# Bias lines by single-pass products, and the order of the opening, of branch A's first scores and of two later stages

## The chip, the cores and the metric

The kernel runs on one core of a Trainium2 chip. The metric is the device time of one execution in microseconds, as the median of three runs. The profile that is quoted is one further execution, taken by the hardware profiler. Engines are named as the profile names them: PE (TensorE, matrix products), PEld (its weight loads), DVE (VectorE), ACT (ScalarE), POOL (GpSimd) and SP (SyncE, which here only issues DMAs).

## What is computed

One encoder layer over two inputs, 1024 rows (the sample) and 256 rows (the prompt) of width 1024. Cut to what matters:

```python
h = _rmsnorm(x, g_mix)
z = h @ w_in                       # q, k, v of two branches, and two gates
o_a, _ = _banded_attention(qa, ka, va, A_WINDOW, 1, rel_bias[:, :A_HEADS], sink)
o_b = _dilated_mixture(qb, kb, vb, rel_bias[:, A_HEADS:])
merged = gates[:, :, 0] * (o_a @ w_branch_a) + gates[:, :, 1] * (o_b @ w_branch_b)
x = x + merged @ w_out
h = _rmsnorm(x, g_mlp)
return x + jnp.square(jax.nn.relu(h @ w_up)) @ w_down
```

A final RMSNorm follows. Branch A is attention in a window of 128 with a sink; it has 8 heads. Branch B mixes three dilated windows with 4 heads each. Both add a bias to the logits, which depends only on the distance of query and key: a table of 32 buckets by 20 heads (`rel_bias`) is looked up by the bucket of the distance.

## The kernel before, in words

Everything runs in one program whose order is written out by hand: within `manual_schedule` each engine carries out its instructions in the order in which the program issues them. Python generators (`turn`, `line`, `fill`, `side` and so on) are advanced step by step with `next`, so that the work of one engine is laced into that of another. DMAs are issued mostly on SP's queue, in program order; a DMA whose destination is not yet free holds up those behind it. Tiles of 4 KB per partition come from a pool of 33 slots ("m"), weights from one of 10 ("w").

**Products.** A float32 operand is split into a high part (rounded to fp32r by ACT, `hi`) and a low part (the rest, by DVE, `lo`). A product of two such operands is three fp32r products: hi x hi, hi x lo and lo x hi, each a single pass on PE. `split` issues both halves at once; `split_steps` yields between ACT's and DVE's. Products of plain float32 tiles are possible too (`tab`, `ones`, `ident` below); the trace shows two PE records for each of those, and one for an fp32r product. `mm3` and `six` (lines 186 to 193 and 351 to 360) issue the three products over all blocks of the inner dimension; `six` with `late=True` first does all products of the two high parts, then those with the low part of the moving operand, and last those with the low part of the stationary operand.

**The stages, in order.**

1. The opening (lines 670 to 905). Row tiles of x are loaded, squared (`square`, ACT), scaled by 1/rms and g_mix (`scale`, DVE), transposed on PE (`turn`), and split. g_mix arrives as a single row and is spread over all partitions by a product with a row of ones (line 816; the result is `g`). Some transposes of the identity into an unused bank stand ahead of and behind it (lines 812 and 813). Tiles 0 and 1 use `g` straight from its bank (`scale_first`, line 825). The value columns of w_in are split piece by piece (`split_v`, line 699), and `values` (line 766) multiplies: first tiles 0 and 1 together, then tile after tile. In that loop the DVE work of a tile is the low halves, the copies out, and the combinations that the next stage needs.
2. The projections (lines 806 to 1075), by pairs of column blocks (`pair`), with a seven-product scheme for two-by-two blocks (`seven`, `prompt`). Between them runs branch B's attention (`attention_b`), and in the hooks of the first six pairs the bias lines: `line` (line 287) multiplies a table tile `tab` (128 x 128 float32, rows 0 to 31 are rel_bias, row 32 is -1e30, the rest zero) with a matrix of zeros and ones (`hot`), which gives the bias per head for each distance (one bias line of 512, two of 384 and three of 256 columns). It is stored and read back with a skew.
3. Branch A (lines 1075 to 1400). 40 tiles (4 units of two heads, 10 row tiles each) pass through scores, maxima, exponentials, transposes and products with the values. Between them PE does the rest of the gate projection in small steps (`fill`, made by `logits`, line 1155): a step is four products of 512 columns or eight of 256. Line 1323 does 18 such steps ahead of the first score. The blocks whose left side is `h21` need tiles that were stored and are loaded back (`scr_h`) shortly before. `load_unit` loads q, k and v of a unit; it is called for the next unit at the unit's tile 0 (line 1329). `merges_of` loads branch B's rows (`r`, from `scr_b`) on SP's queue and merges them on DVE (lines 1178 to 1245).
4. The merge with the gates (lines 1400 to 1445): 48 jobs. Each loads gate values six jobs ahead (`load_gate`), applies the sigmoid three jobs ahead (ACT) and multiplies on DVE. In four jobs `fetch` loads the next weight on SP's queue (line 1424).
5. w_out, the second norm, the up projection, and the down projection (`Down`, lines 1605 to 1815). The down projection has 28 steps; each takes five row blocks (t = 0 to 4), with twelve products of 512 columns per block. The left sides (`uhi`, `ulo`, `up`) and right sides (`dhi`, `dlo`) of a step are split by ACT and DVE during the step before. Line 1788 calls `six` with `late` in the very first block only.

Of the kernel before, what the change touches and what calls it, by code (L numbers as in the profile page):

```python
# [10 lines left out]
F32 = mybir.dt.float32  # L11
# [4 lines left out]
P = 128  # L16
# [6 lines left out]
HD = 64  # L23
# [73 lines left out]
def encoder_kernel(  # L97
# [156 lines left out]
    nsink = const.tile([P, AH], F32, name="nsink")  # L254
    tab = const.tile([P, P], F32, name="tab")
    nc.gpsimd.memset(tab, 0.0)
# [21 lines left out]
    scr_u = [dram.tile([P, 7, 4, TH], F32, name=f"scr_u{g}") for g in range(FF // P // 8)]  # L278
    lines = {}

    def toeplitz(i, cols, first, lo):
# [4 lines left out]

    def line(i, make):

        h0, n, length, _ = LINES[i][3:]
        first = sum(x[5] for x in LINES[:i])  # L290
        hs = make("z")[:, :length]
        nc.gpsimd.memset(hs, 0.0)
        nc.gpsimd.dma_start(hs[: BUCKETS + 1, :], hot[:, first : first + length])
        yield
        yield
        ps = bank("pv", "line")
        nc.tensor.matmul(ps[:, :length], tab, hs, start=True, stop=True)
        ln = make("z")[:NH, :length]
        nc.vector.tensor_copy(ln, ps[:NH, :length])
        d = dram.tile([n, length], F32, name=f"line{i}")  # L300
        nc.gpsimd.dma_start(d, ln[h0 : h0 + n, :])
        wide = dram.tile([P, n, length], F32, name=f"wide{i}")
        nc.gpsimd.dma_start(wide, d[:, :].unsqueeze(0).to_broadcast([P, n, length]))
        lines[i] = wide
        yield
# [365 lines left out]
    with ExitStack() as pre:  # L671
# [6 lines left out]
        gm = slot("gm")  # L678
        gm_row = slot("row")[:1, :]
        ones = small.tile([1, P], F32, name="ones", tag="ones", bufs=1)  # L680
        nc.vector.memset(ones, 1.0)
        NV = (512, 384)
# [16 lines left out]
        def split_v(v, i):  # L699
            if v == 0:  # L700
                hi, lo = wslot("vhi", (P, 2, 512), F32R), wslot("vlo", (P, 2, 512), F32R)
            else:
                hi, lo = own("v2", (P, 2, 384), F32R, 8), own("v2", (P, 2, 384), F32R, 8)
            split(hi, lo, v_raw.pop((v, i)))
            v_parts[v, i] = hi, lo

        def square(t):
# [14 lines left out]
        def turn(t):  # L722
# [19 lines left out]
            for (hi, _), cols, src in jobs:  # L742
                nc.scalar.activation(hi[:, :, cols], src, AF.Copy)
            for (hi, lo), cols, src in jobs:
                nc.vector.tensor_tensor(lo[:, :, cols], src, hi[:, :, cols].bitcast(F32), op=ALU.subtract)
# [37 lines left out]

        nc.scalar.dma_start(gm_row, g_mix)
        load_x(0)
# [25 lines left out]
        for h in range(3):  # L811
            for _ in range((4, 0, 6)[h]):
                nc.tensor.transpose(idle[:, :P], ident, ident)
            if h < 2:
                ps = bank(("mm", "pv")[h], "g")
                nc.tensor.matmul(ps, ones, gm_row[:, 512 * h : 512 * h + 512], start=True, stop=True)
                spread_gm.append(ps)
# [12 lines left out]
        square(1)  # L830
        scale_first(1)
        next(turns[0])
        split_v(0, 0)
        next(turns[1])
        next(turns[1])
        split_v(0, 1)
        square(2)
        split_v(0, 2)
        for h in range(2):
            nc.vector.tensor_copy(gm[:, 512 * h : 512 * h + 512], spread_gm[h])  # L840
        scale(2)
        next(turns[0], None)
        split_v(0, 3)
        square(3)
# [18 lines left out]
        for t in range(2, NT):  # L863
            if t + 1 < NT:
                next(turns[t + 1])
                next(turns[t + 1])
            if t + 3 < NT:
                square(t + 3)
            if t + 2 < NT:
                scale(t + 2)  # L870
            if t + 1 < NT:
                next(turns[t + 1], None)
            if t < 6:
                split_v(1, t - 2)
            if t > 7:
                next(b0)
            ps = bank("mm", "v")
            values(t, 0, ps)
            evac(t, 0, ps)

        def more():
# [368 lines left out]
    if True:  # L1250
# [70 lines left out]
        for name, shape, n in (("bias", (P, 2, 3 * P), 2), ("pt", (P, 6, P), 2), ("s", (P, 2, 3 * P), 4)):  # L1321
            a3(name, shape, n)
        steps_of(fill, 18)
        for i in range(0, len(order) + 4, 2):
            for j in range(2):
                pieces = []
                if i < len(order):
                    u, t = order[i + j]
                    if t == 0 and u < 3:
                        units[u + 1] = load_unit(u + 1), load_bias(u + 1, lambda name, shape: a3(name, shape, 2))  # L1330
# [83 lines left out]
        for i, (x, b, c) in enumerate(jobs):  # L1414
# [8 lines left out]
            open_gate(i + 3)  # L1423
            if i in (1, 4, 22, 26):
                fetch()
            elif i in (5, 8, 33, 35):
                w_as[(5, 8, 33, 35).index(i)] = weight(0)
            elif i in (38, 40, 42, 44):
                prepare()
# [174 lines left out]
    class Down:  # L1604
# [4 lines left out]
        def make(self, name, shape=(P, 2, 512), dt=F32):  # L1609
            return self.late.tile(list(shape), dt, name=name, tag="l4", bufs=8)  # L1610
# [165 lines left out]
        def go(self):  # L1776
            with tc.tile_pool(name="down", bufs=1) as self.late:
                for s, (n, g) in enumerate(JOBS):
# [6 lines left out]
                    for t in range(5):  # L1785
                        ps = self.bank(n, t, g % 2 == 0)
                        six(ps, self.rights[n, g], [self.at(n, g, t, k) for k in range(4)],
                            g % 2 == 0 and n not in (2, 3), g % 2 == 1 and n not in (1, 2), late=s + t == 0)
                        next(side, None)
# [171 lines left out]
```

## Time and profile before

| | |
|---|---|
| median of three runs | 1675.86 us (1675.23 to 1676.54) |
| profiled execution | 1676.28 us |
| its span, first to last instruction | 1673.6 us |
| PE busy | 1660.3 us (99%) |
| PEld busy | 1408.6 us (84%) |
| DVE busy | 980.7 us (59%) |
| ACT busy | 733.3 us (44%) |
| POOL busy | 429.4 us (26%) |
| granted PE clock, mean | 0.999 |

The span starts with the first instruction; about 2.7 us of the profiled execution lie outside it. The stages by time: the opening runs to about 116 us, the projections to 525, branch A to 664, the gates' merge to about 750, w_out and the up projection to 1284, the down projection to the end. A row of the order of time reads: start in us, duration in us, engine, line, operation, destination <- sources, shape, count; in brackets stands how long the engine had been idle before it and what it waited for. Rows of the same line in sequence are merged (x4). A matmul's own duration contains its latency; two neighbours overlap, and what one costs is the distance between the starts. In the list of waits the columns are: waiting engine, tile and line, then what it waited for, with the sum in us, how often, and the longest. Rows of the chain of waits (the work that ended last, followed back from the end) hold start, length and what it was.

### The profile page before, as it was taken

What the parts mean: (1) busy time and instruction counts of PE and PEld (TensorE: products, weight loads), DVE (VectorE), ACT (ScalarE), POOL (GpSimd) and SP (SyncE); (2) the same over time, 40 slices, a digit from 0 to 9 for tenths busy, and PEclk for the clock granted to TensorE, in tenths of its full rate; (3) what the DMA queues carried; (4) which work ended last, traced back from release to release, by engine and by line L of the source; (5) the groups of instructions that cost most, each with busy time, mean ns of one, the idle gap of its engine ahead of it and who ended that gap; (6) DMA issues with size and microseconds to landing.
All of it is one profiled execution on the core that took longest, in us unless ns stands there. A gap on an engine that the chain in (4) does not pass through costs nothing.

```text
span 1673.6 us, 27177 instructions
## 1 busy us (share of the span) xinstructions
PE 1660.3 (99%) x10342; PEld 1408.6 (84%) x10342; DVE 980.7 (59%) x1662; ACT 733.3 (44%) x1586; POOL 429.4 (26%) x399
## 2 busy tenths in 40 slices
PE   9999999999999999999999999999999999999998
PEld 7898888888888888888888888888888888888886
DVE  7634554554452586666578545455457867666575
ACT  7232553544442677544275333333334333333345
POOL 0210122111111222000100456555555412314140
PEclk9999999999999999999999999999999999999999
DMA  6315666664546953545121543343347845633333
GB/s 239 118 55 123 169 186 179 197 195 138 152 120 170 270 177 120 205 139 201 38 89 59 160 161 124 118 161 130 112 160 269 293 131 179 205 101 107 119 119 126
DMA packets 228116, 255.86 MB, mean 153 GB/s; under 512 B 30184, under 2 KB 158652, under 8 KB 227858
## 3 DMA queue, kind: packets, MB, share of 16 engines
q1 hardware_dynamic: 218224, 228.00, 43.1%
q0 software_dynamic: 8384, 23.51, 4.4%
q10 hardware_dynamic: 1378, 2.63, 0.4%
q8 instruction: 81, 1.33, 0.3%
q14 instruction: 49, 0.40, 0.1%
HBM read 168.58 MB, written 90.73 MB: 155 GB/s over the span
## 4 chain that ended last, share of the span: by engine, by line
PE 93%; DMA 3%; DVE 1%; issue 1%; ACT 1%; SPq 0%; POOL 0%; DVEq 0%; ACTq 0%; POOLq 0%
PE dn L357 21%; PE x L357 20%; PE mm L191 14%; PE z L357 10%; PE v L773 6%; PE pv L357 5%; PE y L357 5%; PE mm L357 5%; PE pv L594 1%; PE pv L1140 1%; PE sc L549 1%; PE pt L337 1%; PE tr L346 1%; DMA q<-scr_qa 1%; DMA r<-scr_b 1%
## 5 line engine op out<-in xcount | busy, mean ns | idle before, releaser
L357 PE MATMUL dn<-dhi,ulo 128*128 128x512 f32 x448 | 173.7, 389 | 0.7 <-DVE ulo L185 0.7
L357 PE MATMUL dn<-dhi,uhi 128*128 128x512 f32 x448 | 173.8, 389 | 0.0
L357 PE MATMUL dn<-dlo,uhi 128*128 128x512 f32 x448 | 173.8, 389 | 0.0
L357 PE MATMUL x<-chi,wlo 128*128 128x512 f32 x424 | 166.7, 393 | 0.0
L357 PE MATMUL x<-clo,whi 128*128 128x512 f32 x424 | 165.7, 391 | 0.0
L357 PE MATMUL x<-chi,whi 128*128 128x512 f32 x424 | 165.0, 389 | 0.0
L316 DVE TENSOR_TENSOR wlo<-ta,whi 128x1024 fp32r<-128x1024 f32 x30 | 55.2, 1839 | 160.3 <-ACT whi L314 160.3
L316 DVE TENSOR_TENSOR wlo<-raw,whi 128x1024 fp32r<-128x1024 f32 x60 | 89.4, 1489 | 89.4 <-ACT whi L314 89.4
L391 POOL TENSOR_TENSOR tb<-raw 128x512 f32<-128x512 f32 x16 | 21.1, 1318 | 338.1 <-DMA raw<-in_w_up_dram 212.3
L615 POOL DMA_DIRECT2D scr_b<-o x72 | 39.1, 547 | 250.0 <-ACT o L606 196.0
L357 PEld LDWEIGHTS dn<-dhi,ulo 128*128 128x128 f32 x448 | 84.1, 188 | 18.7 <-DVE ulo L185 1.2
L357 PEld LDWEIGHTS dn<-dlo,uhi 128*128 128x128 f32 x448 | 84.1, 188 | 17.4
L357 PEld LDWEIGHTS dn<-dhi,uhi 128*128 128x128 f32 x448 | 84.0, 188 | 17.3
L185 DVE TENSOR_TENSOR ulo<-uraw,uhi 128x1024 fp32r<-128x1024 f32 x56 | 90.1, 1628 | 10.9 <-ACT uhi L184 10.9
L357 PEld LDWEIGHTS x<-chi,wlo 128*128 128x128 f32 x424 | 79.8, 188 | 17.2 <-issue 1.5
L357 PEld LDWEIGHTS x<-chi,whi 128*128 128x128 f32 x424 | 79.6, 188 | 17.0
L357 PEld LDWEIGHTS x<-clo,whi 128*128 128x128 f32 x424 | 79.8, 188 | 15.0 <-DVE clo L316 0.4
L1643 POOL TENSOR_TENSOR t<-raw,t 128x1024 f32<-128x1024 f32 x16 | 46.9, 2949 | 144.1 <-DMA raw<-in_w_down_dram 144.1
L1799 DVE TENSOR_TENSOR v<-v,dn 128x512 f32<-128x512 f32 x90 | 59.5, 681 | 40.5 <-PE dn L357 37.6
L565 ACT ACTIVATE s<-s,st 128x128 f32<-128x128 f32 (+1 forms) x120 | 52.0, 435 | 49.3 <-DVE st L561 49.2
L357 PE MATMUL dn<-dhi,up 128*128 128x512 f32 x224 | 73.5, 389 | 0.0
L357 PE MATMUL z<-chi,wlo 128*128 128x512 f32 x184 | 71.9, 391 | 0.0
(354 smaller groups left out, 4599.3 us busy)
## 6 DMA issues: line engine op xcount, KB each, us to landing
scr_u<-u SPq DMA_DIRECT2D x112, 320.0 KB, 2.6
uraw<-scr_u SPq DMA_DIRECT2D x56, 512.0 KB, 4.4
raw<-in_w_in_dram SPq DMA_DIRECT2D x33, 512.0 KB, 5.6
raw<-in_w_up_dram SPq DMA_DIRECT2D x32, 512.0 KB, 5.5
raw<-in_w_down_dram SPq DMA_DIRECT2D x28, 512.0 KB, 5.9
sg<-scr_g SPq DMA_DIRECT2D x32, 256.0 KB, 5.3
uraw<-scr_u SPq DMA_DIRECT2D x28, 256.0 KB, 4.3
v<-scr_v SPq DMA_DIRECT2D x96, 64.0 KB, 2.7
```

What stands on the lines that cost most here:

```text
L185: nc.vector.tensor_tensor(lo, src, hi.bitcast(F32), op=ALU.subtract)
L191: nc.tensor.matmul(ps, a, b, start=i == 0, stop=i == len(seq) - 1)
L316: nc.vector.tensor_tensor(lo, src, hi.bitcast(F32), op=ALU.subtract)
L337: nc.tensor.transpose(ps[:, HD * k : HD * k + HD], src[r, :], ident[r, r])
L346: nc.tensor.transpose(ps[:, P * i : P * (i + 1)], xn[t][:, P * k : P * (k + 1)], ident)
L357: nc.tensor.matmul(ps, a, b, start=first and i == 0, stop=last and i == len(seq) - 1, skip_group_check=True)
L391: eng.tensor_tensor(tb[:, 0], b12, b11, op=ALU.subtract)
L565: nc.scalar.activation(d, d, AF.Exp, bias=st[:, x, h : h + 1], accum_out=st[:, x, 2 + h : 3 + h])
L615: nc.gpsimd.dma_start(scr_b[first : first + step * (nq - 1) + 1 : step, i, g, :], o[p0 : p0 + nq, c + x, :])
L773: nc.tensor.matmul(ps[:, :n], a, b, start=k == 0 and j == 0, stop=k == KC - 1 and j == 2)
L1643: (eng or nc.gpsimd).tensor_tensor(o, a, b, op=ALU.subtract)
L1799: nc.vector.tensor_tensor(v, v, ps, op=ALU.add)
```

## The change

Eight things change.

- **Bias lines.** After tile 2 of the opening `tab` is split into `tab_hi` and `tab_lo` (two constants). `line` multiplies both with `hot`, whose tile is now declared fp32r: two single-pass products that accumulate in one bank, in place of one float32 product. `tab` itself becomes one of the 33 slots.
- **g_mix.** The row is loaded into the last partition of a full tile, whose other partitions DVE clears with two memsets. The product uses the last column of the identity, broadcast, in place of the row of ones, so it is 128 x 128 by 128 x 512 and not 1 x 128 by 1 x 512.
- **Warm-up.** The identity products around it are now plain products and no transposes, and 3 and 2 instead of 4 and 6.
- **Order of the opening.** The high half of the first value weights is issued ahead of the high halves of tile 0; the low half stands after two of tile 0's four low halves; the other two come after tile 1's transposes.
- **Fill.** 16 instead of 18 steps ahead of branch A's first score.
- **Units.** The next unit and its bias are loaded at tile 4 and no longer at tile 0.
- **Fetch.** The fourth fetch of the merge stands in job 31 and no longer in job 26.
- **Down projection.** `late` holds for the first row block of every step.

```diff
-    tab = const.tile([P, P], F32, name="tab")
+    tab = slot("tab")[:, :P]
...
+    tabs = [const.tile([P, P], F32R, name=name) for name in ("tab_lo", "tab_hi")]
...
-        hs = make("z")[:, :length]
-        nc.gpsimd.memset(hs, 0.0)
+        hs = make("z", (P, 512), F32R)[:, :length]
+        nc.gpsimd.memset(hs.bitcast(F32), 0.0)
...
-        nc.tensor.matmul(ps[:, :length], tab, hs, start=True, stop=True)
+        for i, t in enumerate(tabs):
+            nc.tensor.matmul(ps[:, :length], t, hs, start=i == 0, stop=i == 1)
...
-        gm_row = slot("row")[:1, :]
-        ones = small.tile([1, P], F32, name="ones", tag="ones", bufs=1)
-        nc.vector.memset(ones, 1.0)
+        gm_row = slot("row")
+        nc.scalar.dma_start(gm_row[P - 1 :, :], g_mix)
+        nc.vector.memset(gm_row[:HD, :], 0.0)
+        nc.vector.memset(gm_row[HD : P - 1, :], 0.0)
+        last_one = ident[:, P - 1 :].to_broadcast([P, P])
...
-            split(hi, lo, v_raw.pop((v, i)))
             v_parts[v, i] = hi, lo
+            return split_steps(hi, lo, v_raw.pop((v, i)))
...
-            for (hi, lo), cols, src in jobs:
+            for i, ((hi, lo), cols, src) in enumerate(jobs):
+                if (t, i) == (0, 2):
+                    yield
                 nc.vector.tensor_tensor(lo[:, :, cols], src, hi[:, :, cols].bitcast(F32), op=ALU.subtract)
...
-        nc.scalar.dma_start(gm_row, g_mix)
...
-            for _ in range((4, 0, 6)[h]):
-                nc.tensor.transpose(idle[:, :P], ident, ident)
+            for _ in range((3, 0, 2)[h]):
+                nc.tensor.matmul(idle[:, :P], ident, ident, start=True, stop=True)
             if h < 2:
                 ps = bank(("mm", "pv")[h], "g")
-                nc.tensor.matmul(ps, ones, gm_row[:, 512 * h : 512 * h + 512], start=True, stop=True)
+                nc.tensor.matmul(ps, last_one, gm_row[:, 512 * h : 512 * h + 512], start=True, stop=True)
...
         scale_first(1)
+        first_v = split_v(0, 0)
+        next(first_v)
         next(turns[0])
-        split_v(0, 0)
+        run(first_v)
         next(turns[1])
+        next(turns[0])
         next(turns[1])
...
+            if t == 2:
+                split(tabs[1], tabs[0], tab)
...
-        steps_of(fill, 18)
+        steps_of(fill, 16)
...
-                    if t == 0 and u < 3:
+                    if t == 4 and u < 3:
                         units[u + 1] = load_unit(u + 1), load_bias(u + 1, lambda name, shape: a3(name, shape, 2))
...
-            if i in (1, 4, 22, 26):
+            if i in (1, 4, 22, 31):
                 fetch()
...
-                            g % 2 == 0 and n not in (2, 3), g % 2 == 1 and n not in (1, 2), late=s + t == 0)
+                            g % 2 == 0 and n not in (2, 3), g % 2 == 1 and n not in (1, 2), late=t == 0)
```

The other callers of `split_v` now run its generator at once, which is what they did before.

More of the change, by code (lines that the diff above doesn't have):

```diff
@@ L285, in toeplitz, with line @@
         return bass.AP(a.tensor, a.offset + length * lo + zero + first, [[n * length - 1, P], [length, 2], [1, cols]])
-    def line(i, make):
-        h0, n, length, _ = LINES[i][3:]
-        first = sum(x[5] for x in LINES[:i])
-        hs = make("z")[:, :length]
-        nc.gpsimd.memset(hs, 0.0)
+    def line(which, make):
+        h0, n, length, _ = LINES[which][3:]
+        first = sum(x[5] for x in LINES[:which])
+        hs = make("z", (P, 512), F32R)[:, :length]
+        nc.gpsimd.memset(hs.bitcast(F32), 0.0)
         nc.gpsimd.dma_start(hs[: BUCKETS + 1, :], hot[:, first : first + length])
@@ L296, in line @@
         ps = bank("pv", "line")
-        nc.tensor.matmul(ps[:, :length], tab, hs, start=True, stop=True)
+        for i, t in enumerate(tabs):
+            nc.tensor.matmul(ps[:, :length], t, hs, start=i == 0, stop=i == 1)
         ln = make("z")[:NH, :length]
         nc.vector.tensor_copy(ln, ps[:NH, :length])
-        d = dram.tile([n, length], F32, name=f"line{i}")
+        d = dram.tile([n, length], F32, name=f"line{which}")
         nc.gpsimd.dma_start(d, ln[h0 : h0 + n, :])
-        wide = dram.tile([P, n, length], F32, name=f"wide{i}")
+        wide = dram.tile([P, n, length], F32, name=f"wide{which}")
         nc.gpsimd.dma_start(wide, d[:, :].unsqueeze(0).to_broadcast([P, n, length]))
-        lines[i] = wide
+        lines[which] = wide
         yield
@@ L831, in encoder_kernel @@
         scale_first(1)
+        first_v = split_v(0, 0)
+        next(first_v)
         next(turns[0])
-        split_v(0, 0)
+        run(first_v)
         next(turns[1])
+        next(turns[0])
         next(turns[1])
-        split_v(0, 1)
+        run(split_v(0, 1))
         square(2)
-        split_v(0, 2)
+        run(split_v(0, 2))
         for h in range(2):
@@ L842, in encoder_kernel @@
         next(turns[0], None)
-        split_v(0, 3)
+        run(split_v(0, 3))
         square(3)
@@ L873, in encoder_kernel @@
             if t < 6:
-                split_v(1, t - 2)
+                run(split_v(1, t - 2))
             if t > 7:
```

## The prediction

> **What bounds the kernel now.** I read the page first, then who TensorE waits for, then the order of time at each place that the change touches.
>
> ```profile
> span 1673.6 us, 27177 instructions
> PE 1660.3 (99%) x10342; PEld 1408.6 (84%) x10342; DVE 980.7 (59%) x1662; ACT 733.3 (44%) x1586; POOL 429.4 (26%) x399
> ```
>
> ```profile
> ...
> PE sc L1098 <- DVE m L1100: 1.0, 1, 1.0
> PE v L773 <- ACT vhi L184: 0.8, 1, 0.8
> PE dn L357 <- DVE ulo L185: 0.7, 1, 0.7
> PE mm L191 <- DMA hlo<-scr_h: 0.7, 1, 0.7
> ...
> PE mm L191 <- DVE sg L1442: 0.2, 1, 0.2
> ```
>
> TensorE (PE) is busy for 1660.3 of 1673.6 us, so there are two ways to be faster: give it less to do, or remove one of its few waits. The second fence has the rows of its list of waits that matter here (us in total, how often, longest); together they are 3.4 us, and all that PE is not busy is 13.3. So this change can't bring tens of us; each of its parts is aimed at one of these rows or at work on PE. A change of under 0.2% (3.35 us) is about what a measurement of this kernel can't tell from none.
>
> **Opening.** The order of time on PE, ScalarE (ACT) and VectorE (DVE):
>
> ```profile
> 2.52 3.77 PE L816 MATMUL g<-row,ones 1*128 1x512 f32 x4
> 7.55 2.76 PE L346 MATMUL tr<-ident,xn 128*128 128x128 f32 x16
> ...
> 12.40 1.19 PE L773 MATMUL v<-vlo,hhi 128*128 128x512 f32 x4
> 19.80 1.03 PE L346 MATMUL tr<-ident,xn 128*128 128x128 f32 x8
> ```
>
> ```profile
> 6.94 0.29 ACT L712 ACTIVATE sd<-ss,eps 128x1 f32<-128x1 f32 x1
> 8.65 0.66 ACT L743 ACTIVATE hhi<-tr 128x256 fp32r<-128x256 f32 x2 [1.42 <-PE tr L346]
> 10.03 1.06 ACT L184 ACTIVATE vhi<-vraw 128x1024 fp32r<-128x1024 f32 x1
> ```
>
> ```profile
> 0.86 0.17 DVE L681 MEMSET ones<- 1x128 f32 x1
> 6.17 1.41 DVE L825 SCALAR_TENSOR_TENSOR xn<-xt,rs,g 128x512 f32<-128x512 f32 x2
> 9.34 1.58 DVE L745 TENSOR_TENSOR hlo<-tr,hhi 128x256 fp32r<-128x256 f32 x4 [0.26 <-ACT hhi L743]
> 11.12 1.23 DVE L185 TENSOR_TENSOR vlo<-vraw,vhi 128x1024 fp32r<-128x1024 f32 x1 [0.19 <-ACT vhi L184]
> 15.47 1.23 DVE L185 TENSOR_TENSOR vlo<-vraw,vhi 128x1024 fp32r<-128x1024 f32 x1 [0.67 <-ACT vhi L184]
> ...
> 18.00 1.28 DVE L717 SCALAR_TENSOR_TENSOR xn<-xt,rs,gm 128x1024 f32<-128x1024 f32 x1
> ```
>
> ACT stands idle for 1.42 us before its hhi copies at 8.65, and then does vhi behind them at 10.03. The change issues vhi first, so it falls into that hole: from the end of sd (6.94 + 0.29 = 7.23) to about 8.3. PE's first products then need only the hhi of tiles 0 and 1, and no longer wait the 0.8 of the list. On DVE the change puts vlo after two of the four hlo: they take 1.58 / 4, about 0.4 each, from 9.34 to 10.1, and vlo ends at 10.1 + 1.23 = 11.3 in place of 12.35. So the second group of products starts at about 11.35 and not at 12.40: 1.05 us earlier.
>
> Not all of that stays. Behind it DVE does the other two hlo (to 12.1), four hlo of tile 1 (1.6, to 13.7), a vlo (to 14.9), then the vlo that stood at 15.47 behind a wait of 0.67. Its vhi comes earlier too, as one 1.06 activation ahead of it has moved, so the wait shrinks and the vlo ends at about 16.5 in place of 16.70. The copies and the scaling behind it, which end today at 18.00 + 1.28 = 19.28, end at about 19.1. Meanwhile PE would be ready for the transposes of tile 2 at 19.80 - 1.05 = 18.75, so DVE becomes the one that is late, by 0.3 or 0.4. I keep 0.7 of the 1.05.
>
> The g products (the row g_mix spread over 128 partitions) now need two memsets of 1024 columns on DVE, queued behind eps; nothing waits for DVE before 6.17, apart from g. The only DVE memset shown takes 0.17 for 128 columns. The bounds are that fixed 0.17 a piece if length cost nothing, and eight times it, 1.36, if everything scales; the vlo (1.23 for 1024 columns) is the nearest row of that length, but reads two operands, and I take 1.0. They end between 1.2 and 3.6, on my value at 2.9. Today g starts at 2.52 and ends at 6.29, and its second half is first read by the second half of the operation at 6.17 (at about 6.9). A start at 2.9 ends at 6.7: free. At 3.6 it costs 0.5. [...]
>
> The warm-up instructions around g become full fp32 products, and fewer. They are not on the path, which runs from the x tiles over ACT and DVE. But the transposes at 7.55 take 2.76 for 16 (0.173 each) and at 19.80 1.03 for 8 (0.129): the PE clock is still low there. That is a rival below. Opening: -0.7, between -1.3 and +0.3.
>
> After t = 2 the tile `tab` is split: one ACT and one DVE operation of 128 columns, under 0.4 each (the 256-column copies and differences above); PE has 24 products of tile 3 ahead of it, so 0, or 0.4 if that cover is gone. `tab` also takes one of 33 shared slots until then; between -0.2 and +0.5, I take 0.
>
> **Bias lines.** Six products with the table, 2 x 512, 4 x 384 and 6 x 256 columns as the trace counts two records for each:
>
> ```profile
> L297 PE MATMUL line<-z,tab x12: 377/483/595, 132.1 to 279.1; 128*128 128x256 f32 x6, 128*128 128x384 f32 x4, 128*128 128x512 f32 x2
> ```
>
> ```profile
> 278.64 1.02 PE L297 MATMUL line<-z,tab 128*128 128x512 f32 x2
> ...
> 279.74 0.40 PE L357 MATMUL z<-hlo,whi 128*128 128x512 f32 x1
> ```
>
> ```profile
> 24.48 5.46 PE v L773 x24
> ...
> 121.17 2.87 PE mm L357 x24
> ```
>
> The pair of 512 starts at 278.64, one ordinary product follows (left out), and the next starts at 279.74: 1.10 us for the pair and one ordinary product, which takes 5.46 / 24 = 0.228. So the pair costs 0.87, or 1.70 ns a column. All six have 512 + 2 x 384 + 3 x 256 = 2048 columns: 3.5 us. Two fp32r products each cost 2 x 0.228 at 512 columns, 2 x 2.87 / 24 = 0.24 at 256, and about 0.35 at 384: 0.46 + 0.70 + 0.72 = 1.9. PE is never idle around them, so the difference is the gain: -1.6, between -1.3 and -1.9. The memset, the loads of `hot` and the stores stay in their order on POOL.
>
> **Branch A's first scores.** The two waits of this stage, and what stands behind them:
>
> ```profile
> 551.51 0.40 PE L191 MATMUL mm<-hhi,wlo 128*128 128x512 f32 x1
> 552.61 0.50 PE L191 MATMUL mm<-hlo,whi 128*128 128x512 f32 x1 [0.70 <-DMA hlo<-scr_h]
> ```
>
> ```profile
> 566.53 0.38 PE L1098 MATMUL sc<-kk,q 128*128 128x256 f32 x1 [1.01 <-DVE m L1100]
> ```
>
> ```profile
> 564.30 0.16 DVE L1191 TENSOR_TENSOR mm__6203<-r 128x4 f32<-128x4 f32 x1 [2.71 <-DMA r<-scr_b]
> ```
>
> ```profile
> 550.74 3.57 SPq L435 DMA_DIRECT2D q<-scr_qa  x4
> 554.35 4.73 SPq L449 DMA_DIRECT2D qp<-scr_qa  x4
> 559.62 2.33 SPq L1181 DMA_DIRECT2D r<-scr_b  x3
> ```
>
> From product to product there should be 0.228; at 551.51 it is 1.10, so that loss is 0.87; the second I count with its 1.01. The first: the fill work reaches the columns that are reloaded (`hlo`) before they have landed. With 16 and not 18 steps ahead of the scores, two steps of eight 256-column products (8 x 0.12 = 0.96 each) are left to stand between the first scores, so two more groups of four score products (0.18 each, an estimate between 0.12 and 0.228 for their 384 columns) come ahead of the first product with `hlo`: about 1.4 us later: the wait goes, -0.9. The second: DVE stood for 2.71 us at 564.30 for `r`, and its maxima, for which PE's score banks wait, are queued behind. The load of `r` was issued at 559.62, behind eight loads of the next unit (550.74 to 559.08) on SP's queue. Moved from t = 0 to t = 4, they stand behind the first two `r`, which then land some 8 us earlier, before DVE asks at 564.30 - 2.71 = 561.6: -1.0. Unit 1 itself is then issued at about 552 to 562 and its scores come at 576. Together -1.9, between -2.1 and 0.
>
> **Later.** In the merge, `fetch` goes from job 26 to job 31:
>
> ```profile
> 732.16 0.38 SPq L221 DMA_DIRECT2D raw<-in_w_out_dram  x1
> ```
>
> ```profile
> 736.16 1.31 ACT L1378 ACTIVATE sg<-sg,bg 128x256 f32<-128x256 f32 x3 [8.32 <-DMA sg<-scr_g]
> ```
>
> This fetch stood on SP's queue until 732.16, and the gate loads behind it left ACT idle for 8.32. Past it, five more gate loads go first. PE shows 0.2 of it (its list, `sg`): -0.2. In the down projection the products with `ulo` go last in the first row block of every step:
>
> ```profile
> 1597.11 0.39 PE L357 MATMUL dn<-dhi,up 128*128 128x512 f32 x1
> 1598.23 0.50 PE L357 MATMUL dn<-dhi,ulo 128*128 128x512 f32 x1 [0.74 <-DVE ulo L185]
> ```
>
> ```profile
> 1594.76 4.55 DVE L185 TENSOR_TENSOR ulo<-uraw,uhi 128x1024 fp32r<-128x1024 f32 x2
> ```
>
> 1598.23 - 1597.11 - 0.228 = 0.9. The two `ulo` are done at about 1598.2 and 1599.3. Eight products (1.82) now stand ahead of the first and ten (2.28) ahead of the second, so PE asks at 1597.34 + 1.82 = 1599.2 and 1599.6: -0.9. Other steps have no wait, and the reordering costs nothing there.
>
> **Sum.** 0.7 + 1.6 + 1.9 + 0.2 + 0.9 = 5.3 us. The profiled execution took 1676.28, of which 1673.6 is its span; that is 0.42 above the median of 1675.86. So 1676.28 - 5.3 = 1671.0 beside it, and 1670.6 as a median.
>
> **The rivals.**
> The waits of branch A only move. With the loads of units 2 and 3 later, another `r` stands behind them; for: PE has little slack there. Then 1.9 is missing: 1672.5. Chance 0.17.
>
> More comes. If the clock is granted one step earlier, g's 3.77 and the 16 transposes (2.76, against 2.06 at the later rate) shrink, so that DVE's chain starts 0.5 earlier; the opening then keeps its whole 1.05, the lines their 1.9 and branch A its 2.1. [...] The trace so far shows only the two rates. That is 0.5 + 0.35 + 0.3 + 0.2 = 1.35 more: 1669.2. Chance 0.15.
>
> Slower: unit 2's loads come too late.
>
> ```profile
> 570.23 6.25 SPq L435 DMA_DIRECT2D q<-scr_qa  x4
> ```
>
> ```profile
> 603.67 0.28 PE L1098 MATMUL sc<-kk,q 128*128 128x256 f32 x1
> ```
>
> ```profile
> SPq L1181 <- DVE z L1199: 8.7, 1, 8.7
> ```
>
> Today unit 2's loads end at 576.5 and its first score is at 603.67, some 27 us later. If SP first meets the 8.7 us wait of a later `r` and then issues them from 591 on, with the same 14.5 us of issue (from behind `r`, 559.62 + 2.33 = 561.95, to 576.5) and 4.7 to land (as `r`: 559.62 to 564.30), they are there at 610, while PE, some 3 us ahead by then, asks at about 600.5: 1670.6 + 9.5 = 1680.1. It decides once the first of them is issued after 581. Against: today SP issues them at 562 without such a wait, 41 us ahead of need. Chance 0.06.
>
> **Numbers.** Forecast 0.62, so the predicted time is 1670.6. The range is 1668.0 to 1674.0: at the low end the second rival with the opening's bound (0.6 more) and 0.6 for the spread of the three runs, at the high end the first with the opening at +0.3 and half a microsecond of that spread; some 0.15 to 0.2 is outside. Faster by over 0.2% means under 1672.5: most of the forecast, the second rival and nearly half of the first, 0.77. Within 0.2%: 0.17. Slower: 0.06.
>
> **What would show it.** Right: the second group of v products at 11.3 to 11.7; twelve line products in about half the time; no wait for `hlo` near 551, none of DVE for `r` near 564, none for `ulo` near 1592 to 1597. Wrong: g ending after 7.2, transposes of tile 2 still at 19.8, a new wait of PE for kk or q, or DVE waiting for another `r`.

## The result, and the profile after

| | before | after |
|---|---|---|
| median, timed side by side | 1675.68 us (1675.23 to 1679.03, six executions) | 1667.54 us (1666.65 to 1668.34, six executions) |
| ratio | | 0.9948 (95% interval 0.9935 to 0.9961) |
| profiled execution / its span | 1676.28 / 1673.6 us | 1668.34 / 1665.2 us |

The gain is 8.1 us. The forecast was 5.3 and its range reached down to 1668.0, so the sign was right and the size too small. First the head of the profile's page after, then the whole list of what PE waits for (sum in us, how often, longest).

```profile
span 1665.2 us, 27194 instructions
PE 1655.0 (99%) x10342; PEld 1407.0 (84%) x10342; DVE 976.1 (59%) x1664; ACT 734.2 (44%) x1587; POOL 429.5 (26%) x399
```

```profile
PE idle L818 <- POOL ident masks.py:199: 1.5, 1, 1.5
PE tr L348 <- DVE xn L830: 0.5, 1, 0.5
PE tr L348 <- ACT hhi L747: 0.3, 1, 0.3
```

Of the waits that the prediction quoted none is left: no `hlo`, no maxima `m`, no `vhi`, no `ulo`, no `sg`. Where the 8.4 us of the span went is read from the start of the same instruction in both orders of time, stage by stage:

| first PE instruction of the stage | before | after | ahead by | gained in the stage before it | forecast |
|---|---|---|---|---|---|
| x after the value stage | 115.52 | 114.05 | 1.47 | opening 1.5 | 0.7 |
| last group of z products (its first) | 518.00 | 515.02 | 2.98 | bias lines 1.5 | 1.6 |
| first product with obhi | 679.88 | 672.88 | 7.00 | branch A 4.0 | 1.9 |
| first dn | 1284.51 | 1277.10 | 7.41 | merge (fetch) 0.4 | 0.2 |
| last dn | 1666.15 | 1657.70 | 8.45 | down projection 1.0 | 0.9 |

Three terms came out within 0.2. The opening and branch A are both twice what was forecast.

The opening in the order of time after, first on PE, then on DVE and ACT:

```profile
3.18 2.87 PE L821 MATMUL g<-row,ident 128*128 128x512 f32 x4
5.88 0.61 PE L818 MATMUL idle<-ident 128*128 128x128 f32 x4
7.03 1.22 PE L348 MATMUL tr<-ident,xn 128*128 128x128 f32 x8 [0.54 <-DVE xn L830]
8.55 1.29 PE L348 MATMUL tr<-ident,xn 128*128 128x128 f32 x8 [0.29 <-ACT hhi L747]
...
10.91 1.19 PE L779 MATMUL v<-vlo,hhi 128*128 128x512 f32 x4
...
18.30 1.03 PE L348 MATMUL tr<-ident,xn 128*128 128x128 f32 x8
```

```profile
1.05 0.91 DVE L683 MEMSET row<- 64x1024 f32 x1 [0.18 <-issue]
2.21 0.91 DVE L684 MEMSET row<- 63x1024 f32 x1 [0.25 <-issue]
...
9.64 1.22 DVE L318 TENSOR_TENSOR vlo<-vraw,vhi 128x1024 fp32r<-128x1024 f32 x1
...
16.41 1.28 DVE L721 SCALAR_TENSOR_TENSOR xn<-xt,rs,gm 128x1024 f32<-128x1024 f32 x1
```

```profile
7.11 1.04 ACT L316 ACTIVATE vhi<-vraw 128x1024 fp32r<-128x1024 f32 x1
8.06 2.47 ACT L747 ACTIVATE hhi<-tr 128x256 fp32r<-128x256 f32 x8
```

vhi fell into ACT's hole at 7.11 as the prediction said, and the second group of v products started at 10.91, 0.4 earlier than the 11.35 of its working. The g products took 2.87 and not 3.77, and the transposes of x started at 7.03 and not at 7.55. (x6 and x4 of the identity are three and two plain products, two records each; a transpose of before has one.) Tile 2's transposes stand 1.50 earlier, at 18.30. DVE was not late for them: its scaling for tile 2 ended at 16.41 + 1.28 = 17.69, where the prediction had put 19.1.

The pair of line products at 512 columns, after, with the product that follows:

```profile
276.07 0.39 PE L299 MATMUL line<-z,tab_lo 128*128 128x512 f32 x1
276.30 0.39 PE L299 MATMUL line<-z,tab_hi 128*128 128x512 f32 x1
276.53 0.40 PE L359 MATMUL z<-hhi,wlo 128*128 128x512 f32 x1
```

From 276.07 to 276.53 it is 0.46, against 0.87 before; that is the two products at 0.228 of the prediction.

In branch A, SP's queue, and then DVE's first operation on `r`, which before stood for 2.71 us:

```profile
547.89 2.13 SPq L1191 DMA_DIRECT2D r<-scr_b  x2
550.06 2.42 SPq L437 DMA_DIRECT2D q<-scr_qa  x4
552.53 6.83 SPq L451 DMA_DIRECT2D qp<-scr_qa  x4
...
570.30 5.22 SPq L437 DMA_DIRECT2D q<-scr_qa  x4
```

```profile
555.58 0.15 DVE L1201 TENSOR_TENSOR mm__6200<-r 128x4 f32<-128x4 f32 x1
```

The first two loads of `r` are issued at 547.89 and no longer at 559.62, and DVE has no bracket: it doesn't wait. Unit 2's loads are issued at 570.30, as early as before (570.23), so the slower rival has no place here.

In the down projection the first row block of the step that waited before:

```profile
1589.92 1.07 PE L359 MATMUL dn<-dhi,uhi 128*128 128x512 f32 x4
1590.83 1.07 PE L359 MATMUL dn<-dlo,uhi 128*128 128x512 f32 x4
1591.74 1.29 PE L359 MATMUL dn<-dhi,ulo 128*128 128x512 f32 x5
```

Eight products stand ahead of the first with `ulo`, and there is no wait.

### The profile page after: what moved, and what is told of

The parts are those of the page before. It is cut to its first block, busy times and chain, and to the rows that moved or that the text cites. A ratio compares the mean times of both kernels' runs of the same rounds, so it can differ in the third digit from the quotient of the medians.

```text
span 1665.2 us, 27194 instructions
## 1 busy us (share of the span) xinstructions
PE 1655.0 (99%) x10342; PEld 1407.0 (84%) x10342; DVE 976.1 (59%) x1664; ACT 734.2 (44%) x1587; POOL 429.5 (26%) x399
## 4 chain that ended last, share of the span: by engine, by line
PE 97%; DMA 2%; DVE 1%; ACT 0%; SPq 0%; issue 0%; DVEq 0%; ACTq 0%
PE dn L359 23%; PE x L359 20%; PE mm L191 15%; PE z L359 10%; PE v L779 6%; PE pv L359 5%; PE y L359 5%; PE mm L359 5%; PE pv L1150 2%; PE pv L596 1%; PE pt L339 1%; PE sc L551 1%; PE tr L348 1%; PE sc L1108 1%; PE sc L1109 1%; DMA scr_g<-z 0%
## 5 line engine op out<-in xcount | busy, mean ns | idle before, releaser
L359 PE MATMUL dn<-dhi,uhi 128*128 128x512 f32 x448 | 160.7, 389 | 0.0
L359 PE MATMUL dn<-dlo,uhi 128*128 128x512 f32 x448 | 160.6, 389 | 0.0
L359 PE MATMUL dn<-dhi,ulo 128*128 128x512 f32 x448 | 156.1, 389 | 0.0
```

The source lines that it names most:

```text
L359: nc.tensor.matmul(ps, a, b, start=first and i == 0, stop=last and i == len(seq) - 1, skip_group_check=True)
```

## The experiments

Two things were to be explained: why the opening brought 1.5 and not 0.7, and why branch A brought 4.0 and not 1.9. The theory after the result: in the opening the new warm-up brings as much as the new order, since the clock rises earlier; in branch A the early loads of `r` and the 16 fill steps depend on each other, so that each alone does not bring its share. Rivals: the order alone made the whole opening (its upper bound was 1.3); the two edits of branch A are independent, and the rest of the 4.0 is chance of one execution.

The runs were made on three chips, each with the kernel before beside them. It took 1676.03 us (one execution) beside the kernels after with the units at tile 0, with 18 steps, with the old order and with the old warm-up; 1676.17 (median of 21) beside the two edits alone in the kernel before and the two halves of the warm-up; 1675.33 (median of nine) beside the rest. Where one time is given without a range, the kernel was executed once.

### Branch A: the fill steps and the unit's loads, one at a time from the kernel after

```diff
-                    if t == 4 and u < 3:
+                    if t == 0 and u < 3:
```

> The changed kernel with the next unit loaded at tile 0 again. First theory (the place of the loads on SP's queue made DVE wait for r, and through DVE's late queue also caused the small waits later in branch A): DVE waits some 2 to 3 us for r near 560 again, another wait for r comes back near 600, and branch A gets longer by 2 to 3 us (span about 1667.5). Rival (the fill steps did it, the place of the loads is worth only the one wait of 1.0): branch A longer by 1.0 to 1.2, no other wait comes back (span about 1666.3).

Measured: 1673.75 us, span 1672.0. It loses 6.75 us against after, nearly all of it between 552 and 572 us. The order of time there, on DVE and PE, then the busy times of 560 to 570 with the granted clock (the column ahead of the last two), for this kernel and then for after:

```profile
562.09 0.16 DVE L1201 TENSOR_TENSOR mm__6200<-r 128x4 f32<-128x4 f32 x1 [5.98 <-DMA r<-scr_b]
```

```profile
563.22 0.58 PE L1108 MATMUL sc<-kk,q 128*128 128x256 f32 x1 [3.18 <-DVE m L1110]
```

```profile
560.00:570.00 10.00, 6.80 (x80) 6.05 (x80) 5.47 (x23) 4.46 (x14) 1.07 (x2) 0.66 1.03 263
```

```profile
560.00:570.00 10.00, 10.00 (x169) 8.93 (x169) 8.42 (x37) 8.06 (x28) 2.69 (x5) 1.00 0.99 279
```

With 16 steps PE is at the scores 1.9 us earlier, but `r` still stands behind eight loads of the next unit. So DVE waits 5.98 for it and not 2.71, the maxima queued behind are late, and PE stands for 3.18. Then comes something no row of before had shown: in the records of the granted clock it falls to a half at 562.57 and stays there for 6.83 us. Instruction by instruction against after, PE loses 0.34 at 550.12 (a short wait for `hlo`), another 3.45 up to the row at 563.22, and then 2.9 by slow products until 569.12, where the difference is 6.68: nearly the whole 6.75. Both expectations were too small, at 2 to 3 and at 1.0 to 1.2; the wait for `r` of the first came, its second wait near 600 didn't.

```diff
-        steps_of(fill, 16)
+        steps_of(fill, 18)
```

> The changed kernel with 18 fill steps ahead of the first score again. First theory: PE waits for the reloaded hlo near 546 to 549 again, 0.9 to 1.2 us, and nothing else comes back (span about 1666.2). Rival (the fill steps carry the gain of branch A beyond the prediction): 2 to 3 us come back, with waits on DVE m, on the score banks or on merged as in the kernel before (span about 1667.5).

Measured: 1670.71 us, span 1668.8. From the last v product to the first product with obhi it takes 561.44 us, against 559.01 in after: 2.4 more, as the rival expected. (Another 1.1 of the span's 3.6 stands in the opening, which isn't edited here: PE waits for `xn` at 35 and 42 us, and the value stage ends at 115.17 instead of 114.05. So this execution keeps only 0.35 of the opening's gain; the other five with the opening of after end that stage at 114.05 to 114.24.) The list of PE's waits has the wait for `hlo` back, and those small ones that before had too:

```profile
PE mm L191 <- DMA hlo<-scr_h: 0.9, 1, 0.9
...
PE sc L339 <- DVE m L1110: 0.4, 2, 0.2
...
PE mm L1273 <- DVE oblo L1281: 0.3, 1, 0.3
```

### The same two edits, alone, in the kernel before

```diff
-                    if t == 0 and u < 3:
+                    if t == 4 and u < 3:
```

> The kernel before, with the next unit loaded at tile 4 and nothing else changed (18 fill steps stay). Theory 1 (the two edits of branch A depend on each other): the rows r land early and DVE no longer waits for them, PE's waits of 1.17 near 565, 0.6 near 610, 0.74 near 641 and 0.46 near 659 mostly go, those for hlo (0.26 and 0.87 near 549 to 551) stay: about -1.6, so 1674.1. Theory 2 (the prediction's sum, in which the edits add up): -1.0, so 1674.7. Rival: the waits only move, 0.

Measured: 1674.85 us (1673.15 to 1676.85, eleven executions), ratio 0.9987 (0.9978 to 0.9996), about -1.3. The median can't decide between the two theories. In the trace DVE waits for no `r`, PE's wait for `hlo` stays, those near 641 and 659, which theory 1 took to go, stay too, and a wait in the merge that was 0.2 before has grown:

```profile
PE mm L191 <- DVE sg L1442: 0.9, 1, 0.9
PE mm L191 <- DMA hlo<-scr_h: 0.8, 1, 0.8
```

```diff
-        steps_of(fill, 18)
+        steps_of(fill, 16)
```

> The kernel before, with 16 fill steps and nothing else changed (the next unit is still loaded at tile 0). Theory 1: PE comes to the scores 1.9 us earlier while r lands when it did, so DVE waits some 6 us for r and PE some 3.2 us for DVE's maxima; the granted clock falls to a half for about 7 us behind that (3.4 us lost); the hlo wait of 1.1 goes. Together about +2.7 by what the trace of the kernel after with the early load showed: 1678.4. If the clock holds: -0.7 or so, 1675.0. Theory 2 (the edits add up): only the hlo wait goes, -0.9, 1674.8.

Measured: 1677.47 us (1676.37 to 1678.90, eleven executions), ratio 1.0006 (0.9997 to 1.0015): the median is 1.3 above before, and the interval includes no change. The profiled span is 3.0 longer. PE's wait, and the busy times around it with the granted clock:

```profile
565.74 0.39 PE L1098 MATMUL sc<-kk,q 128*128 128x256 f32 x1 [3.17 <-DVE m L1100]
```

```profile
560.00:570.00 10.00, 6.46 (x66) 5.11 (x67) 4.98 (x23) 4.12 (x13) 0.71 (x2) 0.89 1.06 255
570.00:580.00 10.00, 10.00 (x128) 8.71 (x130) 5.68 (x25) 8.14 (x27) 3.38 (x6) 0.94 0.72 183
```

The same wait of 3.2 us, and the same fall of the clock, this time from 567.77, 2.0 us behind the end of the wait, for 3.41 us: theory 1's mechanism, at half its 2.7 in the median. The mean granted clock is 0.997 or 0.998 in all eleven executions of this kernel, and 0.999 in 19 of the 21 of before that ran beside it. So the fall is the rule with this order.

The time from the last v product to the first product with obhi in the six kernels; 1.5 us for the bias lines are added to the three that have the new ones, so that all compare with before:

| | next unit at tile 0 | next unit at tile 4 |
|---|---|---|
| 18 steps, in the kernel before | 564.53 (before) | 562.58 (-1.95) |
| 16 steps, in the kernel before | 566.40 (+1.87) | |
| 18 steps, in the kernel after, + 1.5 | | 562.94 (-1.6) |
| 16 steps, in the kernel after, + 1.5 | 567.25 (+2.7) | 560.51 (after: -4.0) |

Fill alone loses 1.9 to 2.7, the units alone bring 1.6 to 1.95, and both together bring 4.0. The seven profiles with both edits and the new lines differ by 1.0 among themselves (558.70 to 559.73, the longest with a wait for `hlo` of 0.5 again). The two are one edit in two places: the late `r` was hidden by the two fill steps, and only when `r` comes early can the steps be moved behind the first scores. The rival of independent edits is refuted.

That explains the loss by the steps alone, but not why both together bring 4.0: the prediction had both in place and booked 1.9. The rest stands in later rows of before, which it did not count:

```profile
641.17 0.27 PE L337 MATMUL sc<-ident,s 64*128 64x64 f32 x1 [0.15 <-DVE m L1100]
641.65 0.58 PE L337 MATMUL sc<-ident,s 64*128 64x64 f32 x11 [0.21 <-DVE m L1100]
...
659.88 0.44 PE L1263 MATMUL mm<-ident,merged 128*128 128x128 f32 x2 [0.29 <-DVE oblo L1271]
```

From start to start these lose 0.7 and 0.5. All three profiles with 18 steps have them, none of the eleven with 16 or 14 has, whether `r` is early or late. So they go with the steps, which are worth 2.4 once `r` is early (with 1.1 to 1.3 at the `hlo` waits), where 0.9 was booked; the units are worth 1.6 to 1.95, where 1.0 was booked. How two steps fewer at the start remove two losses 90 us later isn't shown.

### Fewer fill steps still

```diff
-        steps_of(fill, 16)
+        steps_of(fill, 14)
```

> The kernel after, with 14 fill steps ahead of branch A's first score. Theory 1: with r landing early there is nothing left to gain, PE's waits in branch A are 0.5 in sum at 16 steps: 0, within 0.3 of the kernel after in branch A. Rival: DVE asks for r 1.9 us earlier again, at about 553.7, and r has not landed by then: PE loses 0.5 to 2, and if it stands for 3 us the clock falls and it loses 3 more.

Measured: median 1667.03 us, ratio to before 0.9957 (0.9943 to 0.9971), five executions; after had 0.9948 (0.9935 to 0.9961), so no difference. From the last v product to the first with obhi it takes 558.71 and not 559.01. DVE asks for `r` before it is there again:

```profile
554.99 0.16 DVE L1201 TENSOR_TENSOR mm__6192<-r 128x4 f32<-128x4 f32 x1 [1.23 <-DMA r<-scr_b]
```

PE has other work over this 1.23, so it costs nothing there. Theory 1's gain of nothing came true, and of the rival the wait for `r`; PE has one new wait, 0.72 for DVE's maxima at 601.85, and the stage is no longer for it. But the reserve is used up, and one of the five executions took 1672.33 us, at a mean granted clock of 0.998 where the others have 0.999; no trace shows what it lost.

### The opening: the order and the warm-up apart

The old order of the opening with the new warm-up:

```diff
-                if (t, i) == (0, 2):
-                    yield
...
-        first_v = split_v(0, 0)
-        next(first_v)
         next(turns[0])
-        run(first_v)
+        run(split_v(0, 0))
         next(turns[1])
-        next(turns[0])
         next(turns[1])
```

> The changed kernel with the first value weights split where they were, behind tile 0's high and low halves; the warm-up stays new. First theory (order and clock each give about half): the transposes of tile 2 start at 19.1 to 19.5 in place of 18.3. Rival (the clock alone moves the chain, since the transposes feed everything behind): they stay below 18.7.

The old warm-up with the new order (the row of ones lies in one of the shared slots):

```diff
-        gm_row = slot("row")
-        nc.scalar.dma_start(gm_row[P - 1 :, :], g_mix)
...
+        gm_row = slot("row")[:1, :]
+        nc.scalar.dma_start(gm_row, g_mix)
+        ones = slot("ones")[:1, :P]
+        nc.vector.memset(ones, 1.0)
...
-            for _ in range((3, 0, 2)[h]):
-                nc.tensor.matmul(idle[:, :P], ident, ident, start=True, stop=True)
+            for _ in range((4, 0, 6)[h]):
+                nc.tensor.transpose(idle[:, :P], ident, ident)
...
-                nc.tensor.matmul(ps, last_one, gm_row[:, 512 * h : 512 * h + 512], start=True, stop=True)
+                nc.tensor.matmul(ps, ones, gm_row[:, 512 * h : 512 * h + 512], start=True, stop=True)
```

> The changed kernel with the one-row product of ones and the 4 and 6 identity transposes again; the order of the opening stays new. The row of ones lies in one of the shared slots. First theory (the full-array products raise the PE clock one step earlier, and that is the part of the opening's gain beyond 0.7): products come at half rate until about 9.3 us, the transposes of tile 2 start at about 19.0 in place of 18.3 (span about 1665.9). Rival (the order alone gives the 1.5): they stay at 18.3 to 18.4.

Measured: the old order 1668.35 us, the old warm-up 1667.65, both with a span of 1665.9 (after: 1665.2). The place to read is tile 2's transposes. The old order, with PE's wait for the late vlo, and then the old warm-up:

```profile
11.70 1.19 PE L777 MATMUL v<-vlo,hhi 128*128 128x512 f32 x4 [0.43 <-DVE vlo L318]
...
19.10 1.04 PE L348 MATMUL tr<-ident,xn 128*128 128x128 f32 x8
```

```profile
2.65 3.75 PE L820 MATMUL g<-row,ones 1*128 1x512 f32 x4
6.32 1.54 PE L817 MATMUL idle<-ident 128*128 128x128 f32 x6
7.66 3.34 PE L348 MATMUL tr<-ident,xn 128*128 128x128 f32 x16
...
19.07 1.04 PE L348 MATMUL tr<-ident,xn 128*128 128x128 f32 x8
```

19.80 with both old, 19.10 and 19.07 with one of them, 18.30 with both new: each brings 0.7 to 0.8, and they add up. (The six profiles with the opening of after have 18.30 to 18.55, so against the slowest of them either brings 0.5 to 0.6.) The order brought just what the prediction kept of it, but by luck: the second group of v products came 0.6 earlier with the old warm-up (11.77 for 12.40) and 0.8 with the new one (10.91 for 11.70), not 1.05, and DVE took none of it back at tile 2. The warm-up, taken at nothing, brought as much again. It works in two ways: the six idle transposes (1.54 us here, ahead of the clock's rise) no longer stand in front of the transposes of x, and these run faster (3.34 us for the 16 here; 1.22 and 1.29 for eight each in after). In the execution with the old warm-up vhi also waited 0.73 for its load, so a little of its 0.77 may be that.

Which half of the warm-up raises the clock, the height of g's products or the idle instructions? Two kernels change one each: the row of ones alone (first, second and fourth piece above, with the idle products left plain), and the idle transposes alone (third piece).

> The kernel after, with g again from a row of ones (products of one row by 512 columns); the identity products stay plain, 3 and 2. Theory A: it is g's products over all 128 rows that let the clock rise early; then it rises at 9 to 10.6 us here, as it did with the whole old warm-up, the 16 transposes of tiles 0 and 1 take about 3 us, and tile 2's transposes stand at about 19.0 (18.30 to 18.55 with the new warm-up). Theory B: it is the identity products being plain products and no transposes; then it rises at 5.0 to 7.1 us and tile 2's transposes stay at 18.3 to 18.6. Theory C: neither alone; the rise lies between, at 7.5 to 8.5.

> The kernel after, with the identity products again as transposes, 4 and 6; g stays a product over all 128 rows. Theory A (g's height decides): the clock rises at 5.0 to 7.1 us and tile 2's transposes stand at 18.3 to 18.6. Theory B (plain products against transposes decides): it rises at 9 to 10.6 us, tile 2's transposes at about 19.0. In both cases six transposes behind g may hold the first transposes of x by up to 0.3.

Measured: 1669.25 us (span 1667.2) and 1667.48 us (span 1665.7); tile 2's transposes at 20.23 and 19.11. When the clock rises to full is in the trace's records of the granted clock. All kernels with one of the four warm-ups together:

| warm-up | executions | the clock is full from (us) |
|---|---|---|
| new: g over 128 rows, 5 plain products | 8 | 4.99, 5.37, 5.58, 5.98, 6.20, 6.59, 6.91, 7.06 |
| old: g over one row, 10 transposes | 4 | 9.28, 10.16, 10.58, 11.40 |
| g over 128 rows, 10 transposes | 1 | 8.88 |
| g over one row, 5 plain products | 1 | 12.95 |

The new warm-up is early in all eight, the old late in all four, and neither half alone reaches the new one's times: so far theory C, but 12.95 and 8.88 lie outside the 7.5 to 8.5 that it gave, and 12.95 is not between the two at all. The rise is not at one time even for one and the same warm-up (the eight new ones lie within 2.07 us, the four old within 2.12), and there is one execution of each half.

What sets the time of the rise within one warm-up isn't shown. The records of the granted clock show lengths alone: the one at full rate holds 1662.29 us in before and 1655.46 in after, 6.83 apart, which is as long as the first fall of branch A and twice the second (3.41). At the first fall PE had been standing for 2.5 us.

The table splits by the height of g: with g over 128 rows the clock is full from 8.88 or earlier in all nine executions, with g over one row from 9.28 or later in all five. That speaks for theory A's reason, the height of g's products, and not for its times: 12.95 lies outside its 9 to 10.6, and 8.88 outside its 5.0 to 7.1. With the ten transposes and g over 128 rows PE stands for 0.60 us ahead of g, waiting for the second memset, a gap that the three plain products cover; whether the rise comes later there for that reason isn't shown.

### The first low half earlier still

```diff
         next(first_v)
-        next(turns[0])
         run(first_v)
+        next(turns[0])
         next(turns[1])
         next(turns[0])
```

> The kernel after, with the first low half of the value weights ahead of all low halves of tile 0 on DVE. Theory 1: vlo ends at about 10.1 and no longer at 10.86, PE's second group of products starts at 10.5 and no longer at 10.91, tile 2's transposes come 0.3 to 0.4 earlier, if the clock rises as early as in the kernel after: 1667.2. Rival: the low halves of tile 0 come 0.7 later and PE waits for them at about 11.4: 0 or +0.3.

Measured: median 1667.28 us, ratio to before 0.9952 (0.9939 to 0.9964), no difference from after. The trace shows the step come true and then lost. PE in the opening and, further down, at the transposes of a later tile:

```profile
10.59 1.08 PE L779 MATMUL v<-vlo,hhi 128*128 128x512 f32 x4
...
41.01 1.06 PE L348 MATMUL tr<-ident,xn 128*128 128x128 f32 x8 [0.19 <-DVE xn L721]
```

Tile 2's transposes came 0.35 earlier (17.95), and at 41.01 PE waits for DVE's `xn` and stands where it stands in after (40.95). So in this execution DVE sets the pace of the value stage there, and what the opening still had to give is taken back within 25 us.

### The other parts

The line products in float32 again, everything else as in after. With them go the split of the table, its two halves, its shared slot and the fp32r declaration of `hot`'s tile (not shown):

```diff
-        for i, t in enumerate(tabs):
-            nc.tensor.matmul(ps[:, :length], t, hs, start=i == 0, stop=i == 1)
+        nc.tensor.matmul(ps[:, :length], tab, hs, start=True, stop=True)
```

> The kernel after, with each bias line as one float32 product again. Theory 1 (the two records of a float32 product are the whole cost): the projections, from the end of the value stage to branch A, take 1.5 us longer, the down projection and branch A the same as in after. Rival: the gain came from the table being split and its slot, or from the loads of the lines: then under 0.5.

Measured: 1668.95 us, span 1667.2. From the last v product to the first score it takes 431.50 us against 429.80: 1.7 more, as theory 1 said. The kernel undoes the split and the slot too, so the sum alone doesn't refute the rival; the place of the loss does. Instruction by instruction against after it grows at the six line products, by 1.5 in all, and by another 0.15 near 350 us. The products are the cost.

The fetch back in job 26, and `late` for the very first row block only (two places, 850 us apart):

```diff
-            if i in (1, 4, 22, 31):
+            if i in (1, 4, 22, 26):
...
-                            g % 2 == 0 and n not in (2, 3), g % 2 == 1 and n not in (1, 2), late=t == 0)
+                            g % 2 == 0 and n not in (2, 3), g % 2 == 1 and n not in (1, 2), late=s + t == 0)
```

> The kernel after, with two edits undone that lie far apart: the fourth fetch back in job 26 (the merge, near 735 us) and late only in the very first row block (the down projection). Theory 1: with branch A some 7 us earlier, the gate loads behind the fetch hold PE longer than the 0.2 of before, as in the two kernels that were before with one edit of branch A each (0.9 and 1.1): 1.0 to 1.5 at that place, and one wait for ulo of 0.9 to 1.0 in the down projection; together +2.2. Theory 2 (the prediction's sum): 0.2 for the fetch, 0.9 for late; +1.1.

Measured: 1669.07 us, span 1667.3. PE at the two places:

```profile
734.80 0.50 PE L191 MATMUL mm<-ohi,wlo 128*128 128x512 f32 x1 [0.78 <-DVE sg L1452]
```

```profile
1591.87 0.50 PE L359 MATMUL dn<-dhi,ulo 128*128 128x512 f32 x1 [0.74 <-DVE ulo L185]
```

The first place loses 1.0 by the start of the next stage, the second 1.05. So the fetch is worth 1.0 in the kernel after, where it was 0.2 in before, and theory 1 had the sum, but not the reason. That PE comes earlier can't be it: the kernel with the fill steps alone comes 1.9 later than before and waits 1.1. In all four profiles with the fetch in job 26 (this kernel, before, and before with either edit of branch A) it stands 52.3 us behind the first product with obhi, so it moves along with PE. What differs is when the gate loads behind it land: ACT's second group of 512-column sigmoids starts 7.3 us behind the fetch in before and 7.9 to 8.3 in the others, later by 0.6 to 1.0, which is what PE's wait gains (0.15 in before; 0.78, 0.89 and 1.15). Why they land later isn't shown.

## Why the prediction was right in sign and too small in size

- **Opening, -0.7: mis-sized, measured -1.5** (1.3 to 1.5 in five of six profiles with this opening, 0.35 in the sixth). The order brought 0.7 to 0.8. The step that failed is "they are not on the path, which runs from the x tiles over ACT and DVE". PE itself was late there, as this row of before shows, which the prediction did not use:

```profile
6.22 1.54 PE L813 MATMUL idle<-ident 128*128 128x128 f32 x6
```

  The idle transposes last until 7.76, and those of x start at 7.55, straight behind them; after, PE waits 0.54 for `xn` instead and starts at 7.03. The warm-up was worth another 0.7 to 0.8, the half that the prediction left to a rival with a chance of 0.15. Also "DVE becomes the one that is late" was too early by a stage: it was not late at tile 2, but at 41 us, as the kernel with the low half first showed.
- **Memsets and g: right.** 0.91 a piece against the 1.0 taken; g started at 3.18 and ended at 6.05, ahead of 6.7; in the two executions whose clock rose last (6.91 and 7.06) it ended at 6.96. The two memsets together took 2 x 0.91 = 1.82.
- **Bias lines, -1.6: right.** 1.5 between the profiles, 1.7 with that part undone.
- **Branch A, -1.9: mis-sized, measured -4.0.** Both mechanisms were right: the `hlo` wait went and so did the one for `r`. The step that failed is "the two waits of this stage": the upper bound of 2.1 was made from those two alone. The smaller waits for m and oblo in PE's list were left out: 0.7 near 641 and 0.5 near 659, which went with the steps, and 0.3 of the 0.6 near 611, which went with either edit. The rest is size: 1.1 and not 0.9 for `hlo`, whose short wait at 549 was left out, and 1.3 and not 1.0 near 565, since these listed waits lost more than their idle time (0.87 for 0.70 at 552.61, 1.3 for 1.01 at 566.53). Also, the two edits were booked apart, though the 18 steps covered for the late `r`; the steps alone make the time no shorter.
- **Fetch, -0.2: right for the one profile it was read from,** 0.4 between the profiles. In the three other profiles with the fetch in job 26 the wait was 0.8 to 1.15, so in the kernel after the edit is worth 1.0.
- **Down projection, -0.9: right,** 1.0 and 1.05.
- **The rivals.** That the waits only move is refuted: counted from start to start, PE loses 4.2 us to stalls in branch A before (1.1 near 550, 1.3 near 565, 0.6 near 611, 0.7 near 641, 0.5 near 659) and 0.5 after. The slower one is refuted by unit 2's loads. "More comes" had its first half right, the clock and the 0.5 of the opening, and gave 1669.2; it missed branch A by the same two waits.

## What to carry to other kernels

Two edits around one wait are priced together: first ask what the work that is moved had been hiding, then what lies behind the wait on the queue. A bound for a stage is the sum of all its losses from start to start, and not of the two largest waits. And a wait on a load that costs 0.2 in one profile can cost 1.0 in the next at the same place of the order: its price is read from more than one profile.

## What the runs showed of the hardware

- With a wait of PE of 3.2 us its clock fell to a half, in two kernels: from 0.65 us ahead of the wait's end for 6.83 us (the units at tile 0 in the kernel after), and from 2.0 us behind it for 3.41 (the fill steps alone in the kernel before). With waits of up to 1.0, in branch A of before, it did not. The second half of that price is in no list of waits: only the granted clock of a narrow window shows it (0.66 from 560 to 570 us in the first of the two, 1.00 in after).
- In the kernel before the clock rose at 9.28, ahead of the first v product at 11.13. PE had till then done nothing but transposes and products of one row, and from 6.29, where g's products end, transposes alone. So a rise without any plain product over 128 rows was seen.
- A memset of 1024 float32 columns took 0.91 us on DVE on 64 as on 63 partitions, and one of 128 columns on one partition 0.17.
